# The last product block of a two-block layer stack, finished in three pieces instead of two, with its output stores on two queues

## The chip, the cores and the metric

The kernel runs on one core of a Trainium2 chip. The metric is device time in microseconds (us) of one execution, as the median of several runs. The profile shows one execution on the hardware, with times from the first instruction of the program.

## The reference

256 tokens of width 2048 pass through an even layer (short convolution, state-space heads, memory attention), an odd layer (latent attention, memory attention), a norm, and then a second block: retention, and a squared-ReLU MLP, with residual additions and a final norm. Only its very end is touched here. Cut to that, it is:

```
h = rms_norm(x, norm2)
u = relu(h @ mlp_w_up) ** 2          # 256 x 8192
x = x + u @ mlp_w_down               # 256 x 2048
out = rms_norm(x, final_norm)        # x * rsqrt(mean(x*x) + 1e-6) * w, per token
```

All of it is float32.

## The kernel before, in words

Every weight streams once from HBM through a chain that is the same for all products. SyncE (SP) starts one transfer of up to 1 MB into a `raw` buffer (`emit_dma`, L325), ScalarE (ACT) writes the rounded "high part" `hi` (L183), VectorE (DVE) writes what is left, `lo` (L161), and TensorE (PE) multiplies (`emit_mm`, L176 through the helper `mm`). Each product is three matmuls: high by high, high by low, low by high. The list `subs` holds the pieces of the stream, two 128-row weight tiles each for the blocks that matter here, and `run_stream` takes them in order. `PLAN` fixes the order of the blocks, so no scheduler decides anything.

The down projection of the MLP is cut into three row groups; the last (`part_i == last_part`) has 20 row tiles of 128, and in each group there are four blocks of 512 output columns, `cb` = 0 to 3. With `lay_b` the activations are the stationary operand (128 tokens of token tile `t`, 0 or 1) and 512 weight columns are the moving one. The two token tiles write the two halves of one PSUM tile `g` of shape [128, 2, 512], which is two banks.

After each of the blocks `cb` = 0, 1, 2 of the last group, `post_down` adds the product to the residual, ACT sums its squares per token into `part`, and DVE multiplies by the gain into `xw[cb, t]`. So when the last block (`cb` = 3) ends, three quarters of the final norm's work is done except for the last factor, 1/rms.

The last block is treated apart. Its first eight pieces are multiplied for both token tiles as usual. The last two pieces (four row tiles) are multiplied first for token tile 0 (`only=0`), then `final_rows(ps, 0)` is written, then the same for token tile 1. `final_rows` makes, for one token tile: the residual sum `x3` from PSUM on DVE (L170); the sum of its squares on ACT (`junk`, L173, into column 3 of `part`) beside the gain product `xw[3, t]` on DVE (L161); the sum of four columns of `part` on DVE (L1376); mean plus epsilon on DVE (L167); the power -1/2 on GpSimd (POOL, L452); the scaling of four `xw` tiles by it, 0, 2 and 3 on DVE (L165) and 1 on ACT (L173); and four stores of 256 KB, all started by SP (L1383).

The program gives each engine its instructions in the order in which they are written, and a wait is put in wherever a tile is read that another engine writes, or written that another engine reads. Such waits go by tile: token tile 1's first matmul after `final_rows(ps, 0)` writes the same tile `g` that DVE's L170 reads.

Of the kernel before, what the change touches and what calls it, by code (L numbers as in the profile page):

```python
# [15 lines left out]
D = 2048  # L16
# [8 lines left out]

# [1 line left out]
# One entry per product block: (key, weight, [(first 128-row tile, tiles) per transfer], columns).  # L27
def rows(n, k0=0):
# [86 lines left out]
def block_kernel(ctx, tc, a, out):  # L115
# [30 lines left out]
    def bank(shape, name):  # L146
        # a PSUM bank for a task; it is given back with rel() once its last reader is emitted
        while free_banks[0] == 0:
            yield
        free_banks[0] -= 1  # L150
        return psb.tile(shape, F32, tag="b", name=nm(name))
# [33 lines left out]

# [1 line left out]
    sq = C([128, 3, 128], "sq")  # L187
# [21 lines left out]

# [1 line left out]
    subs = []  # L211
# [9 lines left out]
    class Feat:  # L221
        # transposed operand: high and low parts, four 128-feature tiles to a unit
        def __init__(self, name):
# [25 lines left out]
        def write_scaled(self, kt, n, src, w):  # L249
            # high parts first, then what they leave  # L250
            for k in range(n):
                act(self.hi(kt + k), src(k), AF.Copy, scale=w(k))
            for k in range(n):
                stt(self.lo(kt + k), src(k), w(k), self.hi(kt + k).bitcast(F32), ALU.mult, ALU.subtract)

    # Products with a stationary weight tile stream the high and low parts of x side by side: the
    # bank of a 128-column tile holds (w_hi x_hi + w_lo x_hi) and (w_hi x_lo), summed on the way out.
    def lay_a(nf):
# [8 lines left out]
    def lay_b(ncols):  # L267
        def f(ps):
            return [("B", ps[:, t, 0:ncols], (0, ncols), t, t) for t in range(2)]
        return f  # L270

    def lay_ukv(ps):
        return ([("A3", ps[:, 0, h * 256:(h + 1) * 256], (h * 128, h * 128 + 128), 0, 0) for h in range(2)]
                + [("B", ps[:, 1, t * 256:(t + 1) * 256], (256, 512), 1, t) for t in range(2)])
# [3 lines left out]
    def merged(post):  # L278
        # both 256-column halves of a 512-column block, added up in SBUF, then its own work on [128, 4, 256]
        def make(key, i):  # L280
            def f(ps):
                low = H([128, 2, 256], F32, "low")
                nc.scalar.copy(low, ps[:, :, 256:512])  # L283
                yield
                if key not in halves:
                    halves[key] = [U([128, 4, 256], F32, "blk"), 0]
                u = halves[key][0]
                tt(u[:, 2 * i:2 * i + 2, :], ps[:, :, 0:256], low, ALU.add)
                halves[key][1] += 1
                if halves[key][1] == 2:  # L290
                    halves.pop(key)
                    yield
                    yield from post(u)
            return f
        return make
# [43 lines left out]
    def emit_mm(m, only=None):  # L339
        s = subs[m]  # L340
        job = s.job
        if s.first and job.ps is None:
            job.ps = psg.tile([128, 2, 512], F32, tag="g", name=nm("g"))
        hv_, lv_ = splits[m]
        for k in range(s.n):
            kt = s.k0 + s.s0 + k
            xh, xl, xb = job.x.hi(kt), job.x.lo(kt), job.x.both(kt)
            for kind, dst, (c0, c1), bk, t in job.layout(job.ps):
                if only is not None and t != only:
                    continue  # L350
# [22 lines left out]
    def run_stream():  # L373
# [15 lines left out]
        for m, s in enumerate(subs):  # L389
# [8 lines left out]
            if m < n - 2:  # L398
# [4 lines left out]
                step_tasks()  # L403
        # the last two pieces run token tile by token tile, so that the first one's tail overlaps
        for t in range(2):
            for m in (n - 2, n - 1):
                emit_mm(m, only=t)
            final_rows(subs[-1].job.ps, t)
        drive(lambda: not tasks)

# [1 line left out]
    def evac_tr(feat, u, kp, ps, wcol):  # L412
# [17 lines left out]
    def tr_plain(dst, src):  # L430
        # dst [128, 4, 256] <- four transposed 128-feature blocks of src [128 tokens, 2, 512]
        held = []
        for hp in range(2):
            ps = yield from bank([128, 2, 256], "trp")
            for i in range(2):
                for t in range(2):
                    h = hp * 2 + i
                    nc.tensor.transpose(ps[:, i, t * 128:(t + 1) * 128], src[:, t, h * 128:(h + 1) * 128], ident)
            held.append(ps)
        yield  # L440
        for hp in range(2):
            nc.scalar.copy(dst[:, hp * 2:hp * 2 + 2, :], held[hp])
            rel()
# [19 lines left out]
    def bcast_rows(dst, rstd):  # L463
        # dst [128, 256]: a per-token column pair laid along the free axis of every partition
        ps = yield from bank([128, 256], "bc")
# [12 lines left out]
    def feat_rstd(dst, sqs, n):  # L478
        # sqs: squares [128, 4, 256] of transposed features; dst [128 tokens, 2]
        acc = sqs[0]  # L480
# [12 lines left out]
    def three(dst, l, r, started, last=False):  # L493
        # dst += l r from high and low parts (lh, ll), (rh, rl)
        for i, (x, y) in enumerate(((l[0], r[0]), (l[0], r[1]), (l[1], r[0]))):
            mm(dst, x, y, start=(i == 0 and not started), stop=(last and i == 2))

    def parts(src, name):
        # high and low parts of [128, 256]
        w = H([128, 2, 256], F32R, name)  # L500
# [60 lines left out]

# [1 line left out]
    xres = {}  # L563
# [110 lines left out]
    def rope_tables():  # L674
        # cosine, signed sine, and room for the layer's 1/rms along the free axis;
        # angle = position * inverse frequency in float32, reduced by whole turns with a four-part 2*pi
        tab = U([128, 3, 256], F32, "tab")
# [39 lines left out]

# [1 line left out]
    dts = C([128, 2, 32], "dts")  # L719
# [30 lines left out]
    def dt_task(raw):  # L750
        # softplus(z) = max(z, 0) + log1p(exp(-|z|)), log1p from log by the ratio u / ((1 + u) - 1)
        z, u, w, m, d = (H([128, 2, 32], F32, "dt") for _ in range(5))
# [31 lines left out]
    def conv(src, dst, wname, bname, nw, K, f0):  # L784
        # dst[f, t] = bias + sum_j w[j] * src[f, t - (K - 1 - j)]
        for f in range(4):
# [27 lines left out]
    def ssd_seg(g, hh, t, cb, segs):  # L814
        # segs[hh, t][k, h, q] = CB[q, k] * exp(sum of da over (k, q]) on k <= q
        b = g * 8 + hh * 4
# [134 lines left out]

    # residual add, statistics, transposed operand of the next product
    def post_res(cb, idx, feat, wcol, fin):
# [17 lines left out]

# [1 line left out]
    # rotary key: high part on both 64-row halves, low part on the first / on the second half only  # L973
    ks = C([128, 3, 256], "ks", F32R)
# [103 lines left out]
    def swap_mul(dst, src):  # L1078
        # the two 32-row halves of each 64-row rotary block change places, times the signed sine
        for i in range(4):  # L1080
# [3 lines left out]
    def post_uq(pr):  # L1084
        def f(ps):
# [11 lines left out]
            tt(xr, v[:, 512:768], xr, ALU.add)  # L1097
            # rotary query: its own 64 rows hold the high part, the other 64 the low part
            qs = H([128, 2, 256], F32R, "qs")
# [34 lines left out]
    def attend(pr, h, q, kk, vv, k0, v1):  # L1134
        # scores of the first 128 queries in columns 0:128, of the others in 256:512
        sc = 192 ** -0.5
# [55 lines left out]

# [1 line left out]
    def fin2():  # L1194
# [124 lines left out]

# [1 line left out]
    r3sq = C([128, 2], "r3sq")  # L1321
# [45 lines left out]

    def final_rows(ps, t):
        xw[3, t] = H([128, 512], F32, "xw")
        x3 = U([128, 512], F32, "x3")  # L1370
        stt(x3, ps[:, t, :], r3sq[:, t:t + 1], xres[3][:, t, :], ALU.mult, ALU.add)
        junk = U([128, 512], F32, "junk")
        act(junk, x3, AF.Square, accum_out=part[:, 0, t, 3:4])
        tt(xw[3, t], x3, gain(3, t), ALU.mult)
        sm, r = S([128, 1]), S([128, 1])
        nc.vector.tensor_reduce(sm, part[:, 0, t, :], AX.X, ALU.add)  # L1376
        rstd_from(r, sm, D, 1)
        for cb in (0, 1, 2, 3):
            if cb != 1:
                ts(xw[cb, t], xw[cb, t], r[:, 0:1], None, ALU.mult)  # L1380
            else:
                act(xw[cb, t], xw[cb, t], AF.Copy, scale=r[:, 0:1])
            nc.sync.dma_start(out[0, t * 128:(t + 1) * 128, cb * 512:(cb + 1) * 512], xw[cb, t])  # L1383

# [5 lines left out]

# [1 line left out]
    def vec4(name, cb):  # L1392
# [10 lines left out]
    for entry in PLAN:  # L1403
# [44 lines left out]
        elif kind == "down":  # L1448
            add_job(entry, hid, lay_b(n), post_down(*rest))
    hooks["out0", 0] = load_x  # L1450
# [70 lines left out]
```

## Time and profile before

| | |
|---|---|
| median of 3 runs | 2682.22 us (2681.39 to 2682.43) |
| the profiled execution, first to last instruction | span 2680.9 us |
| PE busy | 2658.8 us, 99% of the span |
| weight loads (PEld) | 2281.3 us, 85% |
| DVE, ACT, POOL busy | 1639.9, 1301.1, 142.6 us |
| DMA | 488.86 MB at a mean of 182 GB/s, all program transfers on SP's queue |

The profiled execution's own time is given as its span alone, 2680.9 us. That is 1.3 us less than the median of the runs and 0.5 us less than the fastest of them; a run's time also holds what lies around the span. Changes are worked out inside the span and then added to the median. In the tables of the trace, "busy" is the time in which an engine executes something, the brackets say how long an engine sat idle before an instruction and which instruction released it, and PE, DVE, ACT, POOL and SP are the five engines. A matmul's end is modelled, so consecutive matmuls overlap in the list; their starts tell the rate.

### The profile page before, as it was taken

Reading aid. Unit: us, or ns where it says so; the run is one execution under the profiler, and the core shown is the slowest. Engines: PE = TensorE matmul, PEld = TensorE weight load, DVE = VectorE, ACT = ScalarE, POOL = GpSimd, SP = SyncE. Lnnn points to the kernel's source line nnn. Section 1 sums busy time; section 2 is a strip of 40 time slices with the busy share of each in tenths; the row PEclk is TensorE's granted clock in tenths of the full one; section 3 lists DMA queues with packets and bytes.
Section 4 is the critical chain, followed back from the end, with each engine's and each line's share of the span. In section 5 each row is a group of like instructions: output and inputs, shape, how many; then the busy total and the mean of one; then the engine's idle time right before and its main releaser. Section 6 shows DMA issues by size and latency. Waiting matters only on the chain.

```text
span 2680.9 us, 34844 instructions
## 1 busy us (share of the span) xinstructions
PE 2658.8 (99%) x14136; PEld 2281.3 (85%) x14136; DVE 1639.9 (61%) x2066; ACT 1301.1 (49%) x1772; POOL 142.6 (5%) x104
## 2 busy tenths in 40 slices
PE   8999999999999999999999999999999999999998
PEld 6998888888899999888888888888888888888886
DVE  6657787655556888656565555565555545545554
ACT  5556555544445666545444343444455434534543
POOL 4101232000000000000000000000000000000000
PEclk9999999999999999999999999999999999999999
DMA  7454444565545444455445455454555555555553
GB/s 270 170 190 167 157 158 163 184 221 197 180 156 201 147 160 163 176 194 202 176 175 183 176 183 190 175 189 176 175 187 188 189 188 188 188 191 186 190 207 137
DMA packets 74689, 488.86 MB, mean 182 GB/s; under 512 B 8864, under 2 KB 10656, under 8 KB 20384
## 3 DMA queue, kind: packets, MB, share of 16 engines
q1 hardware_dynamic: 74528, 486.64, 50.8%
q8 instruction: 110, 1.80, 0.3%
q14 instruction: 51, 0.42, 0.0%
HBM read 484.51 MB, written 2.10 MB: 182 GB/s over the span
## 4 chain that ended last, share of the span: by engine, by line
PE 97%; DVE 1%; ACT 1%; DMA 0%; issue 0%; POOL 0%; SPq 0%; POOLq 0%; DVEq 0%; ACTq 0%
PE g L176 93%; PE tr L423 1%; PE ro L176 1%; PE at.s L176 1%; DMA raw<-in_mem_v_dram 0%; PE rs L176 0%; PE at.o L176 0%; PE yd L176 0%; DVE lo L161 0%; ACT hi L183 0%; PE seg L176 0%; PE ma.s L176 0%; PE ma.o L176 0%; PE at.t L1166 0%; PE pre L176 0%
## 5 line engine op out<-in xcount | busy, mean ns | idle before, releaser
L161 DVE TENSOR_TENSOR lo<-raw,hi 128x1024 fp32r<-128x1024 f32 (+4 forms) x929 | 1116.3, 1212 | 854.5 <-ACT hi L183 853.4
L183 ACT CAST hi<-raw 128x1024 fp32r<-128x1024 f32 (+4 forms) x929 | 938.5, 1028 | 677.5 <-PE g L176 660.9
L176 PE MATMUL g<-h,hi 128*128 128x512 f32 x3072 | 1073.4, 392 | 1.0 <-DVE qx L161 1.0
L176 PE MATMUL g<-h,lo 128*128 128x256 f32 x3072 | 865.9, 282 | 0.0
L176 PEld LDWEIGHTS g<-h,hi 128*128 128x128 f32 x3072 | 576.7, 188 | 121.3 <-issue 2.1
L176 PEld LDWEIGHTS g<-h,lo 128*128 128x128 f32 x3072 | 580.5, 189 | 1.1
L176 PE MATMUL g<-hi,h 128*128 128x512 f32 (+3 forms) x1472 | 433.7, 373 | 0.0
L176 PE MATMUL g<-hi,hid 128*128 128x512 f32 x1024 | 322.7, 396 | 0.8 <-DVE x L170 0.8
L176 PEld LDWEIGHTS g<-hi,h 128*128 128x128 f32 x1472 | 270.0, 188 | 46.0
L176 PE MATMUL g<-lo,h 128*128 128x512 f32 (+3 forms) x736 | 273.9, 372 | 0.0
L176 PE MATMUL g<-hi,y 128*128 128x512 f32 x768 | 244.5, 397 | 0.0
L176 PEld LDWEIGHTS g<-hi,hid 128*128 128x128 f32 x1024 | 192.3, 188 | 47.8 <-DVE x L170 1.3
L283 ACT COPY low<-g 128x512 f32<-128x512 f32 x100 | 58.7, 587 | 349.2 <-PE g L176 349.2
L176 PE MATMUL g<-lo,hid 128*128 128x512 f32 x512 | 202.5, 395 | 0.0
L176 PEld LDWEIGHTS g<-hi,y 128*128 128x128 f32 x768 | 144.2, 188 | 34.8 <-ACT y L183 0.4
L176 PE MATMUL g<-hi,yr 128*128 128x512 f32 x512 | 162.9, 396 | 0.0
L176 PEld LDWEIGHTS g<-lo,h 128*128 128x128 f32 x736 | 138.4, 188 | 22.4
L176 PE MATMUL g<-lo,y 128*128 128x512 f32 x384 | 151.8, 395 | 0.0
L176 PEld LDWEIGHTS g<-lo,hid 128*128 128x128 f32 x512 | 96.2, 188 | 23.1
L176 PEld LDWEIGHTS g<-hi,yr 128*128 128x128 f32 x512 | 96.2, 188 | 23.0
L176 PE MATMUL g<-lo,yr 128*128 128x512 f32 x256 | 101.2, 395 | 0.0
L176 PEld LDWEIGHTS g<-lo,y 128*128 128x128 f32 x384 | 72.2, 188 | 16.8
(284 smaller groups left out, 2030.5 us busy)
## 6 DMA issues: line engine op xcount, KB each, us to landing
raw<-in_w_in_dram SPq DMA_DIRECT2D x96, 1024.0 KB, 4.8
raw<-in_ret_w_in_dram SPq DMA_DIRECT2D x96, 1024.0 KB, 4.8
raw<-in_mlp_w_up_dram SPq DMA_DIRECT2D x64, 1024.0 KB, 4.8
raw<-in_mlp_w_down_dram SPq DMA_DIRECT2D x64, 1024.0 KB, 4.8
raw<-in_w_out_dram SPq DMA_DIRECT2D x48, 1024.0 KB, 4.8
raw<-in_ret_w_out_dram SPq DMA_DIRECT2D x32, 1024.0 KB, 4.8
raw<-in_w_in_dram SPq DMA_DIRECT2D x12, 704.0 KB, 4.0
raw<-in_mem_k_dram SPq DMA_DIRECT2D x8, 1024.0 KB, 4.9
```

Of the source, the lines that this page charges most:

```text
L161: nc.vector.tensor_tensor(o, x, y, op)
L176: nc.tensor.matmul(o, l, r, start=start, stop=stop, skip_group_check=True)
L183: nc.scalar.copy(hi, x)
L283: nc.scalar.copy(low, ps[:, :, 256:512])
L423: nc.tensor.transpose(ps[:, i, t * 128:(t + 1) * 128], src(t, kp + i), ident)
```

## The change

The last block gets three PSUM tiles of one bank each instead of one of two banks: piece 0 is token tile 0 with all 512 columns, piece 1 is token tile 1 with columns 0 to 255, piece 2 is token tile 1 with columns 256 to 511. This holds for all 20 row tiles of the block, so each row tile now has three matmuls of 512 columns and six of 256, each with its own weight load, instead of six of 512. The last two pieces of the stream run piece by piece, and after each comes `final_piece`. The sum of squares over the first three column blocks, divided by the width and with epsilon, is written ahead (`base`); each piece then adds its own part to it with one instruction. The scaling and the stores come after piece 0 for token tile 0 and after piece 2 for token tile 1. Token tile 1's stores of `cb` 1 and 3 are started by ACT, the others by SP.

```diff
+    def lay_last(ps):
+        return [("B", ps[0], (0, 512), 0, 0), ("B", ps[1], (0, 256), 1, 1), ("B", ps[2], (256, 512), 2, 1)]
...
         if s.first and job.ps is None:
-            job.ps = psg.tile([128, 2, 512], F32, tag="g", name=nm("g"))
+            if job is subs[-1].job:
+
+                job.ps = [psb.tile([128, 512 if i == 0 else 256], F32, tag="b", name=nm("last")) for i in range(3)]
+            else:
+                job.ps = psg.tile([128, 2, 512], F32, tag="g", name=nm("g"))
...
-                if only is not None and t != only:
+                if only is not None and bk != only:
...
-        for t in range(2):
+
+        ps = subs[-1].job.ps
+        for i in range(3):
             for m in (n - 2, n - 1):
-                emit_mm(m, only=t)
-            final_rows(subs[-1].job.ps, t)
+                emit_mm(m, only=i)
+            final_piece(ps[i], i)
...
-    def final_rows(ps, t):
-        xw[3, t] = H([128, 512], F32, "xw")
-        x3 = U([128, 512], F32, "x3")
-        stt(x3, ps[:, t, :], r3sq[:, t:t + 1], xres[3][:, t, :], ALU.mult, ALU.add)
-        junk = U([128, 512], F32, "junk")
-        act(junk, x3, AF.Square, accum_out=part[:, 0, t, 3:4])
-        tt(xw[3, t], x3, gain(3, t), ALU.mult)
-        sm, r = S([128, 1]), S([128, 1])
-        nc.vector.tensor_reduce(sm, part[:, 0, t, :], AX.X, ALU.add)
-        rstd_from(r, sm, D, 1)
+    base = C([128, 2], "base")
+    sqs3 = C([128, 3], "sqs3")
+
+    def final_piece(ps, i):
+        t, c0, c1 = ((0, 0, 512), (1, 0, 256), (1, 256, 512))[i]
+        if c0 == 0:
+            xw[3, t] = H([128, 512], F32, "xw")
+            sm = S([128, 1])
+            nc.vector.tensor_reduce(sm, part[:, 0, t, 0:3], AX.X, ALU.add)
+            ts(base[:, t:t + 1], sm, 1.0 / D, EPS, ALU.mult, ALU.add)
+        x3 = H([128, c1 - c0], F32, "x3")
+        stt(x3, ps, r3sq[:, t:t + 1], xres[3][:, t, c0:c1], ALU.mult, ALU.add)
+        junk = H([128, c1 - c0], F32, "junk")
+        act(junk, x3, AF.Square, accum_out=sqs3[:, i:i + 1])
+        tt(xw[3, t][:, c0:c1], x3, gain(3, t)[:, c0:c1], ALU.mult)
+        stt(base[:, t:t + 1], sqs3[:, i:i + 1], 1.0 / D, base[:, t:t + 1], ALU.mult, ALU.add)
+        if c1 < 512:
+            return
+        r = S([128, 1])
+        nc.gpsimd.tensor_tensor(r, base[:, t:t + 1], mhalf[:, 0:1], ALU.pow)
+        for cb in (1, 0, 2, 3):
+            if cb == 1:
+                act(xw[cb, t], xw[cb, t], AF.Copy, scale=r[:, 0:1])
+            else:
+                ts(xw[cb, t], xw[cb, t], r[:, 0:1], None, ALU.mult)
         for cb in (0, 1, 2, 3):
-            if cb != 1:
-                ts(xw[cb, t], xw[cb, t], r[:, 0:1], None, ALU.mult)
-            else:
-                act(xw[cb, t], xw[cb, t], AF.Copy, scale=r[:, 0:1])
-            nc.sync.dma_start(out[0, t * 128:(t + 1) * 128, cb * 512:(cb + 1) * 512], xw[cb, t])
+            q = nc.scalar if t == 1 and cb in (1, 3) else nc.sync
+            q.dma_start(out[0, t * 128:(t + 1) * 128, cb * 512:(cb + 1) * 512], xw[cb, t])
...
-            add_job(entry, hid, lay_b(n), post_down(*rest))
+            last = rest == (last_part, 3)
+            add_job(entry, hid, lay_last if last else lay_b(n), post_down(*rest))
```

The order of the instructions on the engines differs only in this last block. In the rows below each name has a running number, and the brackets name the engines whose signal an instruction waits for.

On PE, where token tile 0's last matmuls end and token tile 1's begin, this stood before:

```order
L176 MATMUL g_21731<-lo_21843,hid_21256 128x512
L176 MATMUL g_21731<-hi_21842,hid_21256 128x512
L176 MATMUL g_21731<-hi_21838,hid_21255 128x512 [waits DVE_49]
L176 MATMUL g_21731<-lo_21839,hid_21255 128x512
L176 MATMUL g_21731<-hi_21838,hid_21255 128x512 x2
```

And this stands there now, at the same place:

```order
L176 MATMUL last_21733<-lo_21883,hid_21258 128x512
L176 MATMUL last_21733<-hi_21882,hid_21258 128x512
L176 MATMUL last_21734<-hi_21878,hid_21257 128x256
L176 MATMUL last_21734<-lo_21879,hid_21257 128x256
L176 MATMUL last_21734<-hi_21878,hid_21257 128x256 x2
```

The wait for DVE is gone, since token tile 1 writes a tile of its own, and the matmuls behind it are half as wide.

On DVE, from the last scaling of token tile 0 (`xw`, L165) to the end, this stood before (`x` is `x3`, `s` the small per-token columns):

```order
L165 TENSOR_SCALAR xw_21882<-xw_21882,s_21889 128x512
L170 SCALAR_TENSOR_TENSOR x_3565_21915<-g_21731,r3sq,x_5449 128x512 [waits PE_49]
L161 TENSOR_TENSOR xw_21914<-x_3565_21915,fw_3445_21181 128x512 [waits DVE_49]
L1376 TENSOR_REDUCE s_21920<-part 128x1 [waits Activation_49]
L167 TENSOR_SCALAR s_21923<-s_21920 128x1 [waits DVE_49]
L165 TENSOR_SCALAR xw_21406<-xw_21406,s_21921 128x512 [waits Pool_49]
L165 TENSOR_SCALAR xw_21768<-xw_21768,s_21921 128x512
L165 TENSOR_SCALAR xw_21914<-xw_21914,s_21921 128x512
```

And this stands there now:

```order
L165 TENSOR_SCALAR xw_21934<-xw_21934,s_21944 128x512 [waits DVE_49]
L1384 TENSOR_REDUCE s_21967<-part 128x1
L167 TENSOR_SCALAR base<-s_21967 128x1 [waits DVE_49]
L170 SCALAR_TENSOR_TENSOR x_3567_21970<-last_21734,r3sq,x_5451 128x256 [waits PE_49]
L161 TENSOR_TENSOR xw_21966<-x_3567_21970,fw_3445_21183 128x256 [waits DVE_49]
L170 SCALAR_TENSOR_TENSOR base<-sqs_98,base 128x1 [waits Activation_49]
L170 SCALAR_TENSOR_TENSOR x_3569_21988<-last_21735,r3sq,x_5451 128x256 [waits PE_49]
L161 TENSOR_TENSOR xw_21966<-x_3569_21988,fw_3445_21183 128x256 [waits DVE_49]
L170 SCALAR_TENSOR_TENSOR base<-sqs_98,base 128x1 [waits Activation_49]
L165 TENSOR_SCALAR xw_21408<-xw_21408,s_21994 128x512 [waits Pool_49]
L165 TENSOR_SCALAR xw_21784<-xw_21784,s_21994 128x512
L165 TENSOR_SCALAR xw_21966<-xw_21966,s_21994 128x512 [waits DVE_49]
```

All of token tile 1's work, the two sums made ahead included, stands behind token tile 0's scalings, and it is eight instructions before the wait for POOL where it was four.

On ACT, token tile 1's squares, its scaling and what follows now read as below; before, ACT had one square of 512 columns there, one scaling and no DMA, and SP started all eight stores:

```order
L173 ACTIVATE junk_21972,sqs_98<-x_3567_21970 128x256 [waits DVE_49]
L173 ACTIVATE junk_21990,sqs_98<-x_3569_21988 128x256 [waits DVE_49]
L173 ACTIVATE xw_21589<-xw_21589,s_21994 128x512 [waits Pool_49]
L1403 DMA out_dram<-xw_21589 128x512 [waits Activation_49]
L1403 DMA out_dram<-xw_21966 128x512 [waits DVE_49]
```

Two of token tile 1's stores have moved here, behind ACT's own scaling.

## Rows read from the trace of the kernel before

**Rows 1.** The page's head.

```profile
span 2680.9 us, 34844 instructions
```

**Rows 2.** Chain of waits, from 2640 us to the end: start us, us, what.

```profile
2639.92 28.25 PE g L176 x121
...
2668.19 0.76 DVE x L170
```

**Rows 3.** Timeline of PE, 2667 us on: start us, us, instruction [idle before, releaser].

```profile
2667.06 0.63 PE L176 MATMUL g<-hi,hid 128*128 128x512 f32 x2
2667.52 0.40 PE L176 MATMUL g<-lo,hid 128*128 128x512 f32 x1
2667.76 0.40 PE L176 MATMUL g<-hi,hid 128*128 128x512 f32 x1
2669.00 0.50 PE L176 MATMUL g<-hi,hid 128*128 128x512 f32 x1 [0.84 <-DVE x L170]
...
2671.66 0.40 PE L176 MATMUL g<-hi,hid 128*128 128x512 f32 x1
```

**Rows 4.** Timeline of DVE, 2669 us on, same columns.

```profile
2669.73 0.16 DVE L1376 TENSOR_REDUCE s<-part 128x1 f32<-128x4 f32 x1
2669.93 0.15 DVE L167 TENSOR_SCALAR s<-s 128x1 f32<-128x1 f32 x1
2670.73 1.28 DVE L165 TENSOR_SCALAR xw<-xw,s 128x512 f32<-128x512 f32 x3 [0.65 <-POOL s L452]
2672.10 0.75 DVE L170 SCALAR_TENSOR_TENSOR x<-g,r3sq,x 128x512 f32<-128x512 f32 x1
2672.89 0.69 DVE L161 TENSOR_TENSOR xw<-x,fw 128x512 f32<-128x512 f32 x1
2673.64 0.16 DVE L1376 TENSOR_REDUCE s<-part 128x1 f32<-128x4 f32 x1
2673.83 0.15 DVE L167 TENSOR_SCALAR s<-s 128x1 f32<-128x1 f32 x1
2674.64 1.28 DVE L165 TENSOR_SCALAR xw<-xw,s 128x512 f32<-128x512 f32 x3 [0.66 <-POOL s L452]
```

**Rows 5.** Timelines of ACT and POOL, 2672 us on, same columns.

```profile
2672.89 0.63 ACT L173 ACTIVATE junk<-x 128x512 f32<-128x512 f32 x1 [1.43 <-DVE x L170]
...
2674.06 0.55 POOL L452 TENSOR_TENSOR s<-s,mhalf 128x1 f32<-128x1 f32 x1 [3.37 <-DVE s L167]
```

**Rows 6.** Groups by line and shape, whole span: xcount | busy us, mean ns | idle before.

```profile
L170 DVE SCALAR_TENSOR_TENSOR h<-tr,pv,h 128x256 fp32r<-128x256 f32 x32 | 13.3, 476 | 4.3 <-ACT h L173 4.3
...
L173 ACT ACTIVATE junk<-ck 128x288 f32<-128x288 f32 x2 | 0.9, 447 | 0.0
...
L173 ACT ACTIVATE junk<-ck 128x224 f32<-128x224 f32 x2 | 0.8, 392 | 0.0
```

**Rows 7.** PE timeline in an earlier block with 256 columns, then its weight loads' group.

```profile
1068.68 0.28 PE L176 MATMUL g<-hi,ck 128*128 128x256 f32 x1
...
1070.08 0.28 PE L176 MATMUL g<-hi,ck 128*128 128x256 f32 x1
...
L176 PEld LDWEIGHTS g<-hi,ck 128*128 128x128 f32 x13 | 2.2, 188 | 0.0
```

**Rows 8.** Stores: SP's first and last issue of token tile 1; its longest wait; landing.

```profile
2675.16 0.33 SPq L1383 DMA_DIRECT2D out_dram<-xw  x1
...
2676.56 0.40 SPq L1383 DMA_DIRECT2D out_dram<-xw  x1
...
SPq L1517 <- DMA out_dram<-xw: 2.9, 1, 2.9
...
DMA to landing us min/median/max: 2.5/3.1/3.4
```

**Rows 9.** Stretch while token tile 1's stores move: engines' busy us, clock, DMA share, GB/s.

```profile
2676.00:2679.40 3.40, 0.00 (x0) 0.00 (x0) 0.00 (x0) 0.00 (x0) 0.00 (x0) 0.50 0.93 306
```

**Rows 10.** A load of the same size in the crowded start: KB, us to landing.

```profile
mem<-in_mem_dram SPq DMA_DIRECT2D x1, 256.0 KB, 5.2
```

## The prediction

> **What bounds the kernel now.** The chain of waits comes first: near the end it is one run of PE matmuls, 121 of them in 28.25 us, and only from 2668.19 us on does it leave PE, for DVE's residual sum of token tile 0 [rows 2]. The span ends at 2680.9 us [rows 1]. So the change can act in two places: on PE in the last block, where each us counts in full, and in the 12.7 us from 2668.19 us to the end. The forecast needs the timelines of that tail.
>
> On PE, 512-column matmuls start every 0.233 us (2667.06 to 2667.76 us is three steps). After token tile 0's last one, which starts at 2667.76 us, the next starts only at 2669.00 us, idle 0.84 us and released by DVE's read of token tile 0. The last matmul starts at 2671.66 us and ends at 2672.06 us [rows 3]. On DVE, token tile 0 is scaled by three instructions from 2670.73 us to 2672.01 us, and token tile 1's residual sum starts at 2672.10 us [rows 4]. So at 2672 us DVE and PE come free within 0.1 us of each other: **the end hangs on DVE's queue as much as on PE**. From there token tile 1 runs through a serial chain to its first scaling at 2674.64 us [rows 4]. Then its stores: SP issues the first at 2675.16 us and the last at 2676.56 us, and waits 2.9 us for the landing [rows 8]; while they move, the 16 DMA engines are 0.93 busy [rows 9].
>
> **The change part by part.** All sums are against the profiled execution's span of 2680.9 us; the median of the runs shown, 2682.22 us, lies 1.3 us above it, and I add the difference to the median.
>
> *Half-width matmuls.* Over 20 row tiles, 60 matmuls of 512 columns become 120 of 256 with 60 more weight loads. An earlier block shows such matmuls, with a new weight load for each: 12 steps take 1.40 us (1068.68 to 1070.08 us), 0.117 us a step, half of 0.233, though a weight load lasts 0.188 us there [rows 7]. The load is hidden. Rounding in these rows leaves 0.001 us a step: for the 96 half-width matmuls ahead of token tile 0's end at most about 0.1 us. I take +0.1 us.
>
> *PE's stall.* With a tile of its own, token tile 1 does not wait for DVE. PE then has its 24 half-width matmuls done about 2.8 us after 2667.99 us (one step after 2667.76), by 2671.0 us instead of 2672.06 us. That is 1.1 us earlier, but I cost it at nothing: DVE, which reads the result, is late instead. It is busy with token tile 0 until about 2672 us, and every instruction for token tile 1 is queued behind that. If DVE were not there, 1.1 us would be the gain.
>
> *Token tile 0's sums made ahead.* The sum of `part` (start 2669.73 us) and the mean (2669.93 us) become one instruction at 2669.73 us, as the other two run earlier while DVE idles. POOL starts 0.20 us earlier, and so do the scalings: **-0.2 us** for whatever follows on DVE [rows 4].
>
> *Token tile 1 on DVE.* Before, from the start of token tile 0's last scaling (2670.73 us plus two steps of 0.40, so 2671.53 us) to token tile 1's first scaling (2674.64 us) it is 3.11 us [rows 4]. Now I add up the new chain.
> - The last scaling's step 0.40. The sum made ahead 0.20 (its step was 2673.64 to 2673.83 us), its mean 0.15: together 0.75. These two are called ahead, but they stand in the queue behind token tile 0's scalings, so they are on the path.
> - Piece 1's residual sum: 256 columns from PSUM take 0.476 us [rows 6], with 0.03 to the next engine 0.51.
> - Its squares: with 512 columns it was 0.75 from ACT's start (2672.89 us) to the DVE instruction that reads the result (2673.64 us), of which the square itself 0.63 [rows 4, 5]. Between 0.392 us for 224 columns and 0.447 us for 288 [rows 6] a square of 256 takes 0.42: 0.54 in all. The gain product on DVE beside it takes 0.69 at 512 columns [rows 4] and ends sooner at half that width.
> - Adding to `base`: 0.15, by the row of one column, as no row shows this form.
> - Piece 2: 0.51 and 0.54 again.
> - From the last small DVE instruction to POOL 0.23, from POOL's start to the scaling 0.58 [rows 4, 5].
>
> That is 0.75 + 0.51 + 0.54 + 0.15 + 0.51 + 0.54 + 0.23 + 0.58 = 3.81 us, 0.70 more than before. Where neighbours on DVE do not depend on each other, one starts some 0.08 us before the other's end (0.40 steps of 0.48 us instructions, as 1.28 us for three shows), at two places here, so between 0.54 and 0.70; I take **+0.6 us**. The split was to overlap piece 1's tail with piece 2's matmuls, but PE has both done by 2671.0 us, before DVE reaches piece 1 at about 2672 us: only the doubled chain is left.
>
> *Two queues for the stores.* ACT starts two of token tile 1's stores, so SP's issues (0.33 to 0.40 us each, 0.47 apart on average) no longer stand in a row: the last store can go some 0.6 us sooner after the first scaling (at its product's end, 1.28 us, instead of at 1.92 us). But the first issue, SP's for `cb` 0, follows the first scaling as before, and from there 1 MB moves at 306 GB/s with the engines 0.93 busy [rows 9]. A full 1.00 would save 0.07 x 3.4 = 0.24 us. No row shows ACT starting a DMA, so bounds: -0.24 us for a queue that fills every gap, and up to +2.1 us if a first use were slow, by the far row of a 256 KB load that landed in 5.2 us in the crowded start [rows 10] against a median of 3.1 us here [rows 8]. I take 0, since the 0.93 is nearest. The Trainium skill, "DMA: Bandwidth & Descriptors", section "Issuing engines are not separate DMA queues", says that DMAs from several engines end on the same 16 DMA engines, and that starting them from several saves only the sequencer's time; it speaks against a gain here, and the 0.93 of one queue agrees as far as one queue can show it.
>
> **Sum.** +0.1 - 0.2 + 0.6 + 0 = **+0.5 us**: span 2681.4 us, median 2682.7 us. What a measurement of this kernel can tell from no change is about 0.2%, 5.4 us, so this counts as no change.
>
> **The rivals.**
> - *The store issue is the limit* (faster). If the end hung on the last issue and a landing and not on the DMA engines, then token tile 1's last product, ready at 2674.64 + 1.28 = 2675.92 us and now 0.5 later, would be issued at once at 2676.45 us and land in 2.5 us, the shortest here [rows 8], where it took 3.4 after 2676.56 us: 1.0 us less, 2681.2 us. If besides the two halves pipelined on DVE without the extra 0.6 us it would be 2680.6 us. For it: SP issues the last product 0.64 us after it is ready. Against: the 0.93 [rows 9], and for the second part that both halves share one queue on DVE. Chance 0.14.
> - *ACT's queue is slow at its first use* (slower within the band). +2.1 us on top: 2684.8 us. For it: no transfer of the program goes through ACT, so nothing shows it. Against: SP's issues are even and short. Chance 0.08.
> - *Weight loads bind at 256 columns* (slower). If a 256-column matmul had to give its weight load the full 0.188 us instead of the 0.117 us step, the 120 of them would take 120 x 0.071 = 8.5 us more, nearly all of it on PE's path: 2691.2 us. It would be slower by over 0.2% from a step of 0.16 us on. For it: 188 ns is longer than 117 ns. Against: the earlier block runs 0.117 us steps under the same loads [rows 7]. Chance 0.03. The Trainium skill, "TensorE: Matmul & The Clock Gate", section "The mechanism", has a line by which weight loads overlap running matmuls only where their row groups differ (it names a background weight buffer as well); taken alone, that line would make this rival the rule for loads over all 128 rows, and rows 7 contradict it.
>
> My own forecast keeps 0.74, and 0.01 is left for a fast case that I do not see.
>
> **How the numbers follow.** The likeliest case has its own bounds: -0.24 for the stores and -0.1 for DVE and PE below 2682.7 us, +0.2 above, and the three runs of before differ by 1.0 us (the front's table), so about 2681.9 to 2683.7 us. To hold 8 in 10 the range goes on into the first two rivals: **2680.9 to 2684.6 us**. All of it lies within the 0.2% band. Faster by over 0.2% would need 5.4 of the tail's 12.7 us, 0.01; slower is the third rival and what I do not see, 0.04; the same 0.95.
>
> **What would show it.** In the changed profile: (1) PE without a gap at 2668 us, and its last matmul ending near 2671 us; half-width steps of 0.117 us, and the block's end for token tile 0 still near 2668.2 us. (2) Token tile 0's first scaling near 2670.6 us. (3) DVE reaching piece 1's residual sum only near 2672 us, long after its matmuls, and then two rounds of residual sum, squares and sum; token tile 1's first scaling near 2675.1 us instead of 2674.64. (4) Stores from two queues, the DMA share still above 0.9, first issue to last landing still about 4.8 us. Wrong would be: token tile 1's scaling before 2674.6 us (then the chain on DVE overlaps more than I think), a store phase under 4.3 us (then the issue was the limit), a PE step above 0.13 us, or anything that moves before 2640 us.

## The result and the profile after

| | median of the runs, us | ratio to the kernel before, 95% interval |
|---|---|---|
| before | 2682.22 (2681.25 to 2682.81, 5 runs) | |
| changed | 2699.75 (2698.90 to 2699.87, 5 runs) | 1.0064 (1.0053 to 1.0075) |

The change makes the kernel 17.5 us slower, over three times the 5.4 us that the prediction took as no change. The page of the changed kernel: its head, and the DMA queues (packets, MB, share of 16 engines).

```profile
span 2697.1 us, 34970 instructions
...
q1 hardware_dynamic: 74240, 486.12, 50.0%
...
q10 hardware_dynamic: 288, 0.52, 0.1%
```

The span is 16.2 us longer than before [rows 1]; q10 is ACT's new queue with its two stores. The chain of waits near the end (start us, us, what):

```profile
2658.55 25.34 PE last L176 x156
...
2683.91 0.76 DVE x L170
```

Token tile 0's residual sum starts at 2683.91 us, where it started at 2668.19 us [rows 2]. 15.7 us are gone before the tail begins, and the last block itself (`last`) still needs some 25 us from its start to that point. So the loss lies ahead of the change's own code. The view by tile shows where. Its rows give shortest, median and longest duration in ns and the first and last start; first the kernel before:

```profile
L176 PE MATMUL g<-ck,hi x128: 277/280/363, 869.9 to 1071.3; 128*128 128x256 f32 x128
...
L176 PE MATMUL g<-hi,yr x512: 389/396/483, 1488.9 to 1956.3; 128*128 128x512 f32 x171
...
L176 PE MATMUL g<-h,hi x3072: 390/390/505, 151.8 to 2558.4; 128*128 128x512 f32 x192
```

and the changed kernel:

```profile
L176 PE MATMUL g<-ck,hi x128: 277/281/369, 874.2 to 1077.7; 128*128 128x256 f32 x128
...
L176 PE MATMUL g<-hi,yr x512: 392/397/479, 1497.5 to 1967.2; 128*128 128x512 f32 x171
...
L176 PE MATMUL g<-h,hi x3072: 388/394/497, 151.8 to 2573.7; 128*128 128x512 f32 x192
```

The same matmul comes at the same 151.8 us, then 4.3 us later (869.9 to 874.2), 10.9 us later (1956.3 to 1967.2) and 15.3 us later (2558.4 to 2573.7). It is a drift through the whole program, in matmuls that the change does not touch. PE does not wait more for anyone: its busy time grows from 2658.8 to 2676.3 us, by as much as the run. Its steps (from the start of one matmul to the start of the next) are longer. The timeline of PE in the MLP's up products, 16 pairs of one 512-column and one 256-column matmul apart, before:

```profile
2538.69 0.39 PE L176 MATMUL g<-h,hi 128*128 128x512 f32 x1
...
2544.23 0.39 PE L176 MATMUL g<-h,hi 128*128 128x512 f32 x1
```

and changed:

```profile
2553.76 0.39 PE L176 MATMUL g<-h,hi 128*128 128x512 f32 x1
...
2559.36 0.39 PE L176 MATMUL g<-h,hi 128*128 128x512 f32 x1
```

5.54 us become 5.60 us, 3.5 to 4 ns a pair. Over the whole trace the mean steps, leaving out gaps of 300 ns and more, are these: where activations are streamed (`g<-h,hi`, 3072 times) a 512-column step goes from 228.6 to 232.3 ns and the 256-column step behind it from 118.5 to 118.3; where 512 weight columns are streamed (some 5200 times) from 233.3 to 234.3 ns. 3072 x 3.5 + 5200 x 1.0 ns = 16 us, the whole drift of 15.6 us to the start of the last block, within the rounding. The granted clock of the two runs is the same within 0.001.

The tail itself, DVE's timeline of the changed kernel from token tile 0's first scaling on:

```profile
2686.26 1.28 DVE L165 TENSOR_SCALAR xw<-xw,s 128x512 f32<-128x512 f32 x3 [0.65 <-POOL s L1395]
2687.46 0.15 DVE L1384 TENSOR_REDUCE s<-part 128x1 f32<-128x3 f32 x1
2687.64 0.15 DVE L167 TENSOR_SCALAR base<-s 128x1 f32<-128x1 f32 x1
2687.71 0.47 DVE L170 SCALAR_TENSOR_TENSOR x<-last,r3sq,x 128x256 f32<-128x256 f32 x1
2688.22 0.42 DVE L161 TENSOR_TENSOR xw<-x,fw 128x256 f32<-128x256 f32 x1
2688.76 0.16 DVE L170 SCALAR_TENSOR_TENSOR base<-sqs,base 128x1 f32<-128x1 f32 x1
2688.84 0.48 DVE L170 SCALAR_TENSOR_TENSOR x<-last,r3sq,x 128x256 f32<-128x256 f32 x1
...
2689.89 0.16 DVE L170 SCALAR_TENSOR_TENSOR base<-sqs,base 128x1 f32<-128x1 f32 x1
2690.78 1.28 DVE L165 TENSOR_SCALAR xw<-xw,s 128x512 f32<-128x512 f32 x3 [0.72 <-POOL s L1395]
```

From scaling to scaling it is 4.52 us where it was 3.91 us [rows 4]: two rounds of residual sum, squares and sum in a row, as forecast. PE runs on without a gap (half-width steps 0.117 us) and starts its last matmul 1.3 us before DVE takes up token tile 1:

```profile
2683.48 0.52 PE L176 MATMUL last<-hi,hid 128*128 128x512 f32 x2
2683.83 0.28 PE L176 MATMUL last<-lo,hid 128*128 128x256 f32 x1
...
2686.41 0.28 PE L176 MATMUL last<-hi,hid 128*128 128x256 f32 x1
```

The stretch in which token tile 1's stores move (engines' busy us, clock, DMA share, GB/s) reads nearly as before, when it was 0.93 and 306 GB/s [rows 9], though the stores now come from two queues:

```profile
2692.10:2695.60 3.50, 0.00 (x0) 0.00 (x0) 0.00 (x0) 0.00 (x0) 0.00 (x0) 0.50 0.91 300
```

### The profile page after: what moved, and what is told of

Its sections match the earlier page's. It is cut to its first block, busy times and chain, and to the rows that moved or that the text cites. A ratio compares the mean times of both kernels' runs of the same rounds, so it can differ in the third digit from the quotient of the medians.

```text
span 2697.1 us, 34970 instructions
## 1 busy us (share of the span) xinstructions
PE 2676.3 (99%) x14196; PEld 2283.6 (85%) x14196; DVE 1640.1 (61%) x2071; ACT 1300.7 (48%) x1774; POOL 141.3 (5%) x104
## 4 chain that ended last, share of the span: by engine, by line
PE 97%; DVE 1%; ACT 1%; DMA 0%; issue 0%; SPq 0%; POOLq 0%; POOL 0%; DVEq 0%; ACTq 0%
PE g L176 92%; PE last L176 1%; PE tr L431 1%; PE ro L176 1%; PE at.s L176 1%; DMA raw<-in_mem_v_dram 0%; PE rs L176 0%; DVE lo L161 0%; PE at.o L176 0%; PE yd L176 0%; PE seg L176 0%; ACT hi L183 0%; DVE xbc L170 0%; PE ma.o L176 0%; PE ma.s L176 0%
## 5 line engine op out<-in xcount | busy, mean ns | idle before, releaser
L176 PE MATMUL g<-hi,hid 128*128 128x512 f32 x944 | 298.2, 396 | 0.0
L176 PEld LDWEIGHTS g<-hi,hid 128*128 128x128 f32 x944 | 177.8, 188 | 43.3
L176 PE MATMUL g<-lo,hid 128*128 128x512 f32 x472 | 187.1, 396 | 0.0
L176 PEld LDWEIGHTS g<-lo,hid 128*128 128x128 f32 x472 | 88.9, 188 | 21.5
```

The source lines that it names most:

```text
L176: nc.tensor.matmul(o, l, r, start=start, stop=stop, skip_group_check=True)
```

## The experiments

The two new constants, `base` and `sqs3`, are padded to 32 bytes per partition each. They lie in the pool of constants, and the pools follow one another in the scratch memory: raw weights, their high and low parts (`wsp`), constants (`cst`), then the activations of all products (`unit`), the work tiles (`half`) and the small columns (`tiny`). So the change moves every activation tile by 64 bytes and leaves the weights where they were. Theory A is that this move is the cause; theory B is that the longer program or the second queue slows the run. The kernel before, run beside each set of experiments on the same chip, took 2681.9 to 2682.2 us.

**e1: the changed kernel with the old addresses.**

```diff
-    base = C([128, 2], "base")
-    sqs3 = C([128, 3], "sqs3")
+    held = []
...
+        if not held:
+            held.extend([S([128, 2], "base"), S([128, 3], "sqs3")])
+        base, sqs3 = held
```

> The changed kernel, but its two new constants (base and sqs3, 64 bytes per partition together) lie in the pool of small per-token columns at the end of the scratch memory, so that the pools of the operands keep the addresses that they had before the change. Theory A (the 64 bytes move every operand tile of TensorE, and 512-column matmuls on them start some 3.6 ns later): the 15.6 us that are lost before the last block come back, its tail keeps the +0.6 us of the changed kernel: 2682.8 us. Theory B (the longer program or its second DMA queue slows the whole run, wherever the operands lie): 2699.7 us, as the changed kernel.

Measured 2682.77 us (ratio 1.0003, 0.9993 to 1.0013). The drift is gone, with all the new code in place. Theory B falls.

**e2, e3, e4: the kernel before with 64, 32 or 96 unused bytes ahead of the activations.**

```diff
     r3sq = C([128, 2], "r3sq")
+    C([128, 16], "pad")
```

(8 columns for 32 bytes, 24 for 96.)

> The kernel before, with nothing but an unused constant of 64 bytes per partition ahead of the operand pools. Theory A: slower by the 15.6 us of drift, 2697.8 us, the drift even over the run as in the changed kernel. Theory B: no change, 2682.2 us.

> The kernel before with an unused constant of 32 bytes per partition, so that operand tiles begin on a multiple of 64 bytes instead of 32 bytes behind one. Theory A leaves open how the time goes with the address: if what counts is whether rows cross a 64-byte line, it is faster than 2682 us; if each 32 bytes cost half of what 64 cost, 2690 us. Theory B: 2682.2 us.

> The kernel before with an unused constant of 96 bytes per partition, so that operand tiles begin on a multiple of 128 bytes. Theory A: another time than 2682.2 us; at or under 2682 us if the distance to a 128-byte line counts, 2705 us if every 32 bytes add 7.8 us. Theory B: 2682.2 us.

Measured: 64 bytes 2698.67 us (ratio 1.0062, 1.0047 to 1.0077), 32 bytes 2697.54 us (1.0058, 1.0038 to 1.0078), 96 bytes 2691.59 us (1.0036, 1.0021 to 1.0052). One unused constant is enough for the whole loss. The 16 pairs in the run with 64 bytes take 5.60 us, as in the changed kernel:

```profile
2554.07 0.39 PE L176 MATMUL g<-h,hi 128*128 128x512 f32 x1
...
2559.67 0.39 PE L176 MATMUL g<-h,hi 128*128 128x512 f32 x1
```

Neither line crossing nor an even price for each 32 bytes, the two laws named above, fits the three.

**e5: 128 bytes.** (The same edit with 32 columns.)

> The kernel before with an unused constant of 128 bytes per partition ahead of the operand pools, after 32, 64 and 96 bytes gave 2697.5, 2698.7 and 2691.6 us. Theory A1 (what counts is where an operand tile begins within a 128-byte line, and 32 bytes behind a line is the good place): 2682 us again. Theory A2 (no such period; any place but the first is slower): 2690 us or more.

Measured 2683.56 us (1.0005, 0.9994 to 1.0017): the time comes back after 128 bytes, or within 1.5 us of it.

**e6: only the work tiles moved.** A pool of 64 bytes is opened between `unit` and `half`:

```diff
+    pad0 = ctx.enter_context(tc.tile_pool(name="pad0", bufs=1))
+    pad0.tile([128, 16], F32, name="pad0t")
     half = ctx.enter_context(tc.tile_pool(name="half", bufs=N_HALF))
```

> The kernel before with the 64 bytes put behind the pool that holds the activations of all products, so that only the 2 KB work tiles of the later steps (and the small columns) move, and no tile that TensorE reads in a weight product does. Theory A1: the steps of the weight products keep their length, 2682 us. Rival (the move of the work tiles that VectorE and ScalarE write slows TensorE): 2698 us.

Measured 2682.58 us (1.0002, 0.9991 to 1.0014). The work tiles do not matter; the activations do.

**e7, e8: weights and activations moved together, and by different amounts.** The same pool of 64 bytes ahead of `wraw`; in e8 also the 64 bytes in `cst`.

> The kernel before with 64 bytes ahead of everything, the raw weights, their high and low parts, the constants and the activations, so that all move together and their distances stay. Theory A1 (the place of the activations within a line): 2698 us, as with the activations alone moved. Rival A3 (the distance between the weights and the activations counts): 2682 us.

> The kernel before with the weights moved by 64 bytes and the activations by 128, so that the activations keep their place within a 128-byte line. Theory A1: 2682 us. Rival A3 (the distance between weights and activations counts): 2698 us. If the place of the weights counts by itself, another time than both.

Measured: e7 2682.15 us (1.0000, 0.9988 to 1.0011), e8 2698.41 us (1.0062, 1.0039 to 1.0084). This refuted my theory A1, by which the place of the activations within 128 bytes counts. The activations of e7 stand in the place that cost 16 us in e2, and it costs nothing, since the weights moved too; in e8 they stand in the good place and the loss is there. What counts is the **distance between weights and activations**, not the place of either. The 16 pairs take 5.55 us in e7

```profile
2537.54 0.39 PE L178 MATMUL g<-h,hi 128*128 128x512 f32 x1
...
2543.09 0.39 PE L178 MATMUL g<-h,hi 128*128 128x512 f32 x1
```

and 5.60 us in e8:

```profile
2553.74 0.39 PE L178 MATMUL g<-h,hi 128*128 128x512 f32 x1
...
2559.34 0.39 PE L178 MATMUL g<-h,hi 128*128 128x512 f32 x1
```

**e9: without the column halves, old addresses.**

```diff
-        return [("B", ps[0], (0, 512), 0, 0), ("B", ps[1], (0, 256), 1, 1), ("B", ps[2], (256, 512), 2, 1)]
+        return [("B", ps[0], (0, 512), 0, 0), ("B", ps[1], (0, 512), 1, 1)]
...
-        t, c0, c1 = ((0, 0, 512), (1, 0, 256), (1, 256, 512))[i]
+        t, c0, c1 = ((0, 0, 512), (1, 0, 512))[i]
```

(and `range(2)` for the pieces)

> The changed kernel with the old addresses and without the column halves: token tile 1 is one piece of 512 columns with a bank of its own; sums made ahead and two store queues stay. If the halves cost 0.6 us by doubling the chain on VectorE, the time from token tile 0's first scaling to token tile 1's goes from 4.45 us back to about 3.9 us, and the span is 0.2 to 0.3 us under that of the kernel before: 2681.8 us. If the bank of its own (no wait of TensorE) is worth the 1.1 us by which TensorE ends earlier, it is 2680.9 us. If two store queues help by themselves, the time from the first store's issue to the last landing is under 4.5 us; if not, 4.8 us.

Measured 2682.00 us (1.0000, 0.9989 to 1.0010). DVE's two scalings:

```profile
2669.86 1.28 DVE L165 TENSOR_SCALAR xw<-xw,s 128x512 f32<-128x512 f32 x3 [0.72 <-POOL s L1397]
...
2673.66 1.28 DVE L165 TENSOR_SCALAR xw<-xw,s 128x512 f32<-128x512 f32 x3 [0.66 <-POOL s L1397]
```

3.80 us apart, against 4.45 us in e1 with the halves (2669.54 to 2673.99 us) and 3.91 us before: the halves cost 0.65 us. The 0.1 us that e9 gains on before is less than the sums made ahead give (2.35 us from token tile 1's residual sum to its scaling, where it was 2.54), so PE's earlier end brings nothing. From SP's first store of token tile 1 (2674.18 us) to the span's end (2680.0 us) it is 5.8 us, against 5.7 us before [rows 1, 8]: the second queue brings nothing either.

**e10: the halves on a longer end.** The changed kernel with the old addresses as in e1, and the last four pieces of the stream run piece by piece:

```diff
-            if m < n - 2:
+            if m < n - 4:
...
-            for m in (n - 2, n - 1):
+            for m in range(n - 4, n):
```

> The changed kernel with the old addresses, but the last four pieces of the stream (eight row tiles instead of four) run piece by piece. Token tile 0 is then done some 5.6 us before TensorE ends, so VectorE is free when the first column half comes, and its chain lies beside the second half's matmuls. If the halves lost only because VectorE was busy with token tile 0, token tile 1's first scaling follows TensorE's end by 2.0 us instead of 4.1 us, and the time is 1.6 us under the kernel before: 2680.4 us. If the doubled chain costs wherever it stands, 2682.8 us.

Measured 2680.08 us (0.9992, 0.9983 to 1.0002), on DVE:

```profile
2667.74 1.28 DVE L165 TENSOR_SCALAR xw<-xw,s 128x512 f32<-128x512 f32 x3 [0.72 <-POOL s L1397]
...
2670.99 0.48 DVE L170 SCALAR_TENSOR_TENSOR x<-last,r3sq,x 128x256 f32<-128x256 f32 x1 [0.60 <-PE last L176]
...
2672.87 1.28 DVE L165 TENSOR_SCALAR xw<-xw,s 128x512 f32<-128x512 f32 x3 [0.66 <-POOL s L1397]
```

Now the second half's residual sum waits for PE, and the scaling follows it by 1.88 us. Counted from the last block's first matmul to the end of the span, it is 36.5 us here, 38.2 before and 38.6 in e1. By the interval the 2 us of the medians are not clear of no change, but the traces show 1.7 of them. How much is the split's was not tested, since no run has the longer end without the halves. An estimate: in e9, with one piece of 512 columns, the scaling follows the residual sum by 2.35 us, here by 1.88, so the halves are worth some 0.5 us of the 1.7, and the rest comes from the longer end, which lets DVE finish token tile 0 before PE ends. So the split can pay, once DVE has nothing of token tile 0 left, but by this estimate it is the smaller part.

**e11, e12: using the distance.** For the blocks that stream 512 weight columns, the weights' parts are written 8 columns (32 bytes) into buffers widened from 1024 to 1056 columns, with `N_HALF` 14 instead of 15 to make room; e11 makes this edit in the kernel before, e12 in that of e10.

```diff
-        hi = wsp.tile([128, 1024], F32R, tag="hi", name=nm("hi"))
+        hi = wsp.tile([128, 1056], F32R, tag="hi", name=nm("hi"))
...
+        o = 8 if s.job.key[0] in ("mv", "out0", "out1", "v", "g", "rout", "down") else 0
...
-        hv_ = hi[:, 0:n * nc_].rearrange("p (k c) -> p k c", c=nc_)
+        hv_ = hi[:, o:o + n * nc_].rearrange("p (k c) -> p k c", c=nc_)
```

(`lo` likewise)

> The kernel before, with the high and low weight parts of the products that stream 512 weight columns over stationary activations (memory values, out, value, gate, retention out and down blocks) written 32 bytes further into their buffers, so that they lie 0 instead of 32 bytes, modulo 128, from the activations; the other products keep 32. To make room, the work pool has 14 instead of 15 buffers. Theory A3 (the distance between weights and activations sets the steps, each form of product with a best place of its own): the 512-column steps of these blocks go from 233.3 to 232.4 ns as in the run with 96 bytes, some 5000 of them, so 4.8 us less: 2677.2 us. If the distance acts on the run as a whole, or the smaller pool makes waits, 2682 us or more.

> Both of the last two together, the longer end in pieces and the weights of those blocks 32 bytes further: if both hold, 4.8 + 1.6 us less than the kernel before: 2675.6 us; if neither, 2682 us or more.

Measured: e11 2668.86 us (0.9952, 0.9937 to 0.9967), e12 2668.57 us (0.9949, 0.9932 to 0.9966). Both beat both kernels, by more than I expected: 120 steps of these blocks take 28.00 us before

```profile
2592.16 0.63 PE L176 MATMUL g<-hi,hid 128*128 128x512 f32 x2
...
2620.16 0.63 PE L176 MATMUL g<-hi,hid 128*128 128x512 f32 x2
```

and 27.63 us in e11:

```profile
2579.24 0.62 PE L176 MATMUL g<-hi,hid 128*128 128x512 f32 x2
...
2606.87 0.62 PE L176 MATMUL g<-hi,hid 128*128 128x512 f32 x2
```

That is 233.3 ns to 230.3, not to 232.4. The 1.6 us of e10 are in e12's trace, from the last block's start to the end (36.6 us, against 37.8 in e11 and 38.2 before), but not in the medians, which differ by 0.3 us: in e12's trace the last block starts 1.1 us later than in e11's (2630.3 for 2629.2 us), as much as runs with the old addresses differ among themselves (2641.6 to 2642.8 us).

**e13, e14: the wider buffers alone, and with distance 0 everywhere.** The edit of e11 with `o = 0`, and with `o = 8` for all products.

> The kernel before with its eight weight buffers 4224 instead of 4096 bytes apart and 14 instead of 15 work buffers, the weights at the buffers' start, so that the distance to the activations stays 32 bytes modulo 128. If the distance modulo 128 is the whole law, the 512-column steps stay at 233.3 ns and the time at 2682 us. If the spacing of the buffers (their distance beyond 128 bytes) did the 13.4 us of the run before, 230.4 ns and 2668 us. If the two share it, 2677 us.

> The same with the weights of all products 32 bytes into their buffers, so that the distance is 0 modulo 128 everywhere. If the distance modulo 128 is the whole law, it is the time of the run with 96 bytes ahead of the activations, 2691.6 us. If distance 0 in the 512-column blocks does the gain only with the wider spacing, these steps are 230.4 ns as in the mixed run, while the steps of the other products, which stream activations, rise by some 2 ns each: 2668.9 plus about 12 us, 2681 us.

Measured: e13 2686.14 us (1.0016, 1.0005 to 1.0028), e14 2677.62 us (0.9986, 0.9974 to 0.9997). No forecast of e13's time held, and e14 came out 3.4 us under the nearer of its two. Wider spacing alone loses 4 us; with it, distance 0 brings the weight-streaming steps to 230.4 ns in e11 and e14 alike. So the distance modulo 128 does much of it, but not all: the spacing has a share that depends on the distance.

The runs together (distance: start of the activations minus start of the weights, modulo 128 bytes; steps are means in ns, without gaps of 300 ns and more; the start of the last block is that of its first matmul in the profiled execution):

| run | distance | buffers apart | 512 / 256 columns of activations | 512 columns of weights | last block starts, us |
|---|---|---|---|---|---|
| before | 32 | 4096 | 228.6 / 118.5 | 233.3 | 2642.8 |
| changed | 96 | 4096 | 232.3 / 118.3 | 234.3 | 2658.4 |
| e1 | 32 | 4096 | 228.6 / 118.5 | 233.3 | 2641.7 |
| e2 | 96 | 4096 | 232.3 / 118.3 | 234.3 | 2658.7 |
| e3 | 64 | 4096 | 232.3 / 119.5 | 233.4 | 2658.3 |
| e4 | 0 | 4096 | 230.6 / 120.6 | 232.4 | 2651.5 |
| e5 | 32 | 4096 | 229.3 / 117.7 | 233.3 | 2643.6 |
| e7 | 32 | 4096 | 228.6 / 118.5 | 233.3 | 2641.6 |
| e8 | 96 | 4096 | 232.3 / 118.2 | 234.3 | 2658.4 |
| e11 | 32, weights streamed 0 | 4224 | 229.7 / 118.0 | 230.4 | 2629.2 |
| e13 | 32 | 4224 | 229.7 / 118.1 | 233.6 | 2646.2 |
| e14 | 0 | 4224 | 231.6 / 118.6 | 230.4 | 2637.2 |

## Why the prediction was wrong, and where it was right

**The step that failed** stands in its first paragraph: "So the change can act in two places: on PE in the last block, where each us counts in full, and in the 12.7 us from 2668.19 us to the end." It took the unchanged order of instructions for an unchanged program. The change acts in a third place, through two lines that I put at nothing without naming them: `base` and `sqs3`, 64 bytes that move every activation tile against the weights. By e1 (old addresses, all the new code) and e2 (64 bytes, none of the new code) these 64 bytes are the whole of the 16 us before the last block. The closing list did name what shows it, "anything that moves before 2640 us", yet no rival had a mechanism for it.

Point by point, against its terms:

- *Half-width matmuls, +0.1 us.* They cost nothing that shows. From the last block's start to token tile 0's residual sum it is 25.52 us in the changed kernel and 25.40 before, which looks like the forecast 0.1 us, but by luck: with the old addresses (e1) it is 25.40 us, and with the 64 bytes and none of the half-width matmuls (e2) 25.51 us. The rival of exposed weight loads, the only one with a time beyond the band (2691.2 us), has no part in the loss: the half-width steps are 0.117 us.
- *PE's stall, at nothing.* Right. The gap is gone and PE's last block takes 28.3 us where it took 29.3 (to its last matmul's end); token tile 1's first scaling still comes later, and e9 keeps this without any gain from it beyond the next term.
- *Sums made ahead, -0.2 us.* Right: from the residual sum of token tile 0 to its first scaling 2.35 us (2683.91 to 2686.26), before 2.54; with the old addresses (e1) 2.42 us, so 0.1 to 0.2 us.
- *Token tile 1 on DVE, +0.6 us.* Right: 4.52 us for 3.91. Without the halves it is 3.80 us (e9); with DVE free (e10) the scaling comes 1.9 us after PE's end, in the changed kernel 4.1 us. So the halves cost because both stand in DVE's queue behind token tile 0.
- *Two queues, 0.* Right: 6.3 us from token tile 1's first scaling to the span's end, as before, and 0.91 busy DMA engines. The first two rivals, a store issue that limits and a slow first use of ACT's queue, both fall with these 6.3 us. The Trainium skill, "DMA: Bandwidth & Descriptors", section "Issuing engines are not separate DMA queues", says that starting DMAs from several engines saves only the sequencer's time of starting them; the trace with two queues in use agrees (e9, 5.8 us against 5.7).
- *The sum, +0.5 us.* With the old addresses the last block to the end took 38.58 us against 38.16 before, +0.4. That e1 measured 2682.77 us where the forecast for the change was 2682.7 is no finer proof, since its interval is some 2.7 us to either side. The mechanism of every term that I listed held, and the size to about 0.1 us; the list was short of one. The likeliest case's bounds do not follow from their terms either: -0.34 and +0.2 us give 2682.4 to 2682.9 us, and 2681.9 and 2683.7 add 0.5 us below but 0.8 above.

**What stays open.** Why the distance matters was not measured directly. It acts between the weights and the activations. One reading is that TensorE's own reads of the two, as the two operands of the same stream of matmuls, meet at some distances and miss at others; the other, that its reads meet the work of ACT and DVE on the weight parts. The kept traces speak against the second. A stretch of the MLP's up products in which DVE, ACT and POOL run nothing (busy us of PE, PEld, DVE, ACT, POOL, clock, DMA share, GB/s), and nine pairs inside it, before:

```profile
2533.46:2536.80 3.34, 3.34 (x21) 2.98 (x20) 0.00 (x0) 0.00 (x0) 0.00 (x0) 1.00 0.93 336
...
2533.49 0.39 PE L176 MATMUL g<-h,hi 128*128 128x512 f32 x1
...
2536.61 0.39 PE L176 MATMUL g<-h,hi 128*128 128x512 f32 x1
```

and changed:

```profile
2548.46:2551.85 3.39, 3.39 (x21) 2.99 (x20) 0.00 (x0) 0.00 (x0) 0.00 (x0) 1.00 0.95 346
...
2548.51 0.39 PE L176 MATMUL g<-h,hi 128*128 128x512 f32 x1
...
2551.66 0.39 PE L176 MATMUL g<-h,hi 128*128 128x512 f32 x1
```

3.12 us become 3.15 us with none of the three at work. Over the whole trace, the steps of `g<-h,hi` that have no instruction of these three engines within 0.2 us go from 228.3 ns (360 steps) to 232.1 (362), and in e2 to 232.1; those during which no DMA packet is under way, from 228.6 ns (1017 steps) to 232.2 (1032). The loss is there in full either way. That leaves the reads of the two operands as the likeliest place, by exclusion; how they meet, no run shows.

The Trainium skill, "SBUF — State Buffer", section "SBUF: two separate sides", says that on the engines' side only the port pair that VectorE shares with GpSimd causes contention, and that TensorE never waits for anyone. Taken as the whole of what can slow a read, it would have given the changed kernel the forecast time, and the rows differ: 228.6 to 232.3 ns by 64 bytes of distance. As a statement on waits for other engines it agrees with the idle stretches above.

Nor do the runs give the law: distances are known in steps of 32 bytes, distance 0 gives 232.4 ns with buffers 4096 bytes apart and 230.4 with 4224, and products of 288, 352 and 384 columns were not looked into. In e11 and e14 the weight parts also move against the raw weights and against the start of their own buffers, which no run separates.

## What to carry to other kernels

A diff of the instruction order does not show what a change does to the layout: if a change allocates anything, even 20 bytes, compare where the operand tiles of the bounding engine lie before and after, or give new small tiles a place behind all large pools. When a result differs from a well-supported sum by much more than the part that was edited can hold, line up equal instructions of the two traces; an even drift through untouched code points at the layout, and one unused constant in the old kernel tests it. And splitting a tail into halves pays only where the engine that takes up the halves is through with the first before the second comes (e10), and loses where both wait in its queue (the change): ask which queue the first half stands in, not only when its matmuls end.

## What the runs showed of the hardware that I had not expected

A matmul of 512 float32 columns in a steady stream, with a new weight load each, does not have one step length: its mean step was 228.6 to 232.3 ns with activations streamed and 230.4 to 234.3 ns with weights streamed, 1.6 and 1.7% from best to worst among the places tried, with the same matmuls each time. Moving weights and activations together changes nothing (e7, 228.6 and 233.3 ns as before). Moving the activations by 128 bytes changes the mean steps by under 1 ns (e5), but the means hide more: the steps of `g<-lo,hid` went from 233.3 to 231.0 ns and those of `g<-hi,hid` from 233.4 to 234.5. In this kernel, where TensorE is busy for 99% of the span, these 64 bytes were worth 16 us one way, and a chosen distance with wider buffers 13 us the other.
